# Recurrence gates of a hybrid decoder trunk: from both parts of the activations in separate matmuls to both parts stacked in one contraction

## The chip, the cores and the metric

The program runs on one core of one Trainium2 chip. The metric is device time in microseconds (us) of one execution. Engines are named as in the profile: PE is TensorE's matmul side and PEld its weight loads, DVE is VectorE, ACT is ScalarE, POOL is GpSimd, SP is SyncE, which issues the loads from memory. Every engine works its instructions in the order in which they stand in its own queue, and waits where an operand or a buffer is not yet free.

## The reference

Two layers, 256 tokens, width 1024. Each layer runs a SwiGLU feed-forward block, a mixing block, a second feed-forward block and a gated addition of a per-layer input. The change is in the mixing block, in the gates of its recurrence:

```python
def rg_lru(x, w_a, b_a, w_x, b_x, lam):
    xb = x.reshape(B, S, RNN_BLOCKS, RNN_BW)             # 16 blocks of 64 channels
    r = sigmoid(einsum('bsnc,ncd->bsnd', xb, w_a).reshape(B, S, C) + b_a)
    i = sigmoid(einsum('bsnc,ncd->bsnd', xb, w_x).reshape(B, S, C) + b_x)
    log_a = -RG_C * r * softplus(-lam)
    a = exp(log_a)
    mult = sqrt(-expm1(2.0 * log_a))
    u = mult * (i * x)
    h = associative_scan(h[t] = a[t] * h[t-1] + u[t])
```

So each of 16 blocks of 64 channels has two 64x64 gate matrices of its own. `x` here is the output of a causal convolution over the projected input. The other branch of the mixing block is an attention of 8 heads with q and k normalised per head; both branches go through output projections, are gated and added.

## The kernel before, in words

Activations lie with features on the 128 partitions and the 256 tokens in the free dimension: 8 feature tiles `m` of [128, 256]. All products are made in three terms so that they keep float32 accuracy: a value is split into a part `hi` (float32r) and the rest `lo`, and a product is hi x hi + hi x lo + lo x hi. The helper `mm3` (lines 308 to 310) issues these three matmuls of 256 columns; `mm3m` (lines 313 to 315) the same for token-major results.

Weights come through class `Weights`: SP loads a chunk into `wr`, ACT copies it into `wh` (line 94) and DVE subtracts to make `wl` (line 95), a unit of 1024 columns at a time, at most five units of each alive. A new unit can be written only when PE has finished the unit five before it. The number in a name (`wh107`) is the unit's.

In the mixing block (`mix`) the order written in the program is: projection to the recurrent branch with the convolution behind it (`conv`) and the split of its result `xc` (`split`, lines 524 and 525); the value projection `v` with the gates of tiles 0 to 4 between its chunks; four groups `qk_group` of the q and k projection, tokens on partitions, two for each half of the heads, with gates 5 to 7 in the first group. A qk group ends, for each of its two PSUM banks, with a square on ACT (line 657), a reduction and small steps on DVE and POOL (lines 659 to 663) and a scaling copy out of the bank (line 665).

After the first two qk groups `root` (line 572) takes one square root over all eight gate tiles on ACT, `tq`, with a load of ACT's function table before it; then `scan` multiplies (line 577) and runs the recurrence over the tokens (line 578), eight times each on DVE. Attention goes head by head in four steps: `step_a` transposes q and k and splits them (lines 700 to 704), `step_b` makes the scores `s` and the softmax (lines 717 to 723), `step_c` and `step_d` transpose the weights `pt` and make the output. Between them stand 24 projections called `filler`, each 24 matmuls of 256 columns into one PSUM bank `f`, the first eight of which are the other gate of the recurrent branch.

PSUM has four banks with the tag `mm` and four with `at`, given out in turn: a tile takes over the bank of the tile given out four earlier with its tag, and PE's first matmul into it waits until that one has been read. The first filler takes over the bank of `qk277`, the first bank of the third qk group.

The order on each engine is not the written one: a list scheduler of the framework moves instructions by its own estimate of times, so that a change in one place shifts others.

The gates of tile `m` before the change: for each of the two gates three matmuls with a 128x128 matrix that holds the two 64x64 blocks on its diagonal and zeros elsewhere, into one half each of a bank `g`; then two tanh on ACT (lines 556 and 557), `thr` and `thi`.

Of the kernel before, what the change touches and what calls it, by code (L numbers as in the profile page):

```python
# [16 lines left out]
P = 128  # L17
DEPTH = 2
D = 1024
KT = D // P            # feature tiles of the model width  # L20
S = 256
TT = S // P            # token tiles
FF = 2816
FT = FF // P           # feature tiles of the FFN width
# [4 lines left out]
# columns of the packed per-feature vectors (one column per feature tile)  # L29
# [11 lines left out]
VC = 258               # columns of one chunk of [v | f]  # L41
# [6 lines left out]
class Weights:  # L48
    """Weights in order of use: loaded in chunks, split into float32r parts hi + lo in units."""
# [11 lines left out]
    def load_first(self):  # L61
        """the first chunks in pieces: a list of loads, each to be issued in its place"""
# [34 lines left out]
    def apart(self, ap, n):  # L97
        """weights loaded and split out of turn, into buffers of their own"""
# [20 lines left out]
def trunk(ctx: ExitStack, tc: tile.TileContext, xT, pT, vec, w1i, w1o, wf, wqk, wv, wg, wro, wao, wo, w2i, w2o,  # L119
# [82 lines left out]
    # masks of S' = -S: +BIG where the key comes after the query  # L202
    mask = cp.tile([P, S], F32, name="mask")
    # cumulative sum over tokens: tri[t, t'] = 1 where t <= t'
    tri = cp.tile([P, S], F32R, name="tri")
    # selection columns for the forget bias: row groups (of 32) dk_hi, dk_lo, dq_hi, dq_lo
# [3 lines left out]
    sel = cp.tile([P, 3], F32, name="sel")      # [-lo rows | key rows | query rows]  # L210
# [6 lines left out]
    sp = cp.tile([P, DEPTH, 2, KT], F32, name="sp")   # [4 softplus(-lam) | its negative]  # L217

    def log_sigmoid(o, z, n):
        """o = min(z, 0) - log1p(exp(-|z|)) for [P, n], in steps"""  # L220
# [96 lines left out]
    class Pair:  # L317
        """tiles of [128, hi 256 | lo 256], four in each buffer"""
# [15 lines left out]
        def split(self, k, src, scale=None):  # L334
            """tile k = src (* scale) in two parts"""
# [9 lines left out]
    def mm2(ps, wh, wl, t, first, last):  # L345
        """ps[:, :256] + ps[:, 256:] += weights x activations, of which the second half is hi x lo"""
# [12 lines left out]
    def unit(ps, act):  # L359
        """one output tile [128 features, 256 tokens] from one weight unit of 8 tiles"""  # L360
        tiles(ps, W.next(), act, range(KT))
# [10 lines left out]
    def pair(psa, psb, act, between=None, tiles=tiles):  # L372
        """two units at the start of a stage, whose last input tile comes late"""
# [566 lines left out]
def _layout(inputs):  # L940
# [24 lines left out]
    for i, t in enumerate((g["rg_wa"], g["rg_wx"])):  # L965
        t = t.reshape(L, KT, 2, 64, 64)
        for b in range(2):
            wg[:, b * 64:(b + 1) * 64, :, i, b * 64:(b + 1) * 64] = t[:, :, b].transpose(0, 2, 1, 3)
# [49 lines left out]
```

## Time and profile before

| what | value |
|---|---|
| median of three runs | 1327.73 us (1326.57 to 1328.20) |
| span of the profiled execution | 1326.2 us |
| TensorE | busy 1313.2 us, 99% of the span, 8610 matmuls |
| VectorE | busy 1077.3 us, 81% |
| ScalarE | busy 814.1 us, 61% |

The profile gives the span from the first to the last instruction; the runs also hold what lies around it, so the fastest run is 0.4 us and the median 1.5 us above the span. A busy share over the whole span says little about one stage; the rows below are from the stage that the change touches, which in the first layer lies between about 205 and 440 us and in the second between about 857 and 1092 us.

### The profile page before, as it was taken

How to read it: one execution, taken by the hardware profiler on the slowest of the kernel's cores; microseconds unless marked ns; L12 is line 12 of the kernel's file. 1: busy time of each engine (PE TensorE's matmuls, PEld its weight loads, DVE VectorE, ACT ScalarE, POOL GpSimd, SP SyncE). 2: the span in 40 equal slices, each digit the busy share in tenths (PEclk: the TensorE clock that was granted, in tenths of full speed). 3: DMA queues.
4: the chain of work that ended last, by engine and by line, in shares of the span. 5: the costliest groups of instructions: out<-in, count | busy, mean ns of one | idle time of the engine just before them, and what ended most of it. 6: DMA issues, size and time to landing. Idle time of an engine off the chain costs nothing.

```text
span 1326.2 us, 22448 instructions
## 1 busy us (share of the span) xinstructions
PE 1313.2 (99%) x8610; PEld 1198.0 (90%) x8610; DVE 1077.3 (81%) x2139; ACT 814.1 (61%) x1467; POOL 35.8 (3%) x43
## 2 busy tenths in 40 slices
PE   8999999999999999999999999999999999999997
PEld 7888899989999888889988888998899998888897
DVE  7998768889768799867789877698997678998766
ACT  6665655867655666556556556578676556655643
POOL 1000000020000000000000000000200000000000
PEclk9999999999999999999999999999999999999998
DMA  7554565445345455456455546654443455554550
GB/s 278 199 186 159 194 229 190 159 151 207 142 145 191 156 212 190 165 173 240 168 189 188 185 141 226 219 189 159 170 177 139 154 183 203 184 187 153 207 192 33
DMA packets 37835, 239.16 MB, mean 180 GB/s; under 512 B 4320, under 2 KB 4960, under 8 KB 14944
## 3 DMA queue, kind: packets, MB, share of 16 engines
q1 hardware_dynamic: 37296, 237.21, 50.6%
q8 instruction: 68, 1.11, 0.3%
q10 hardware_dynamic: 432, 0.52, 0.1%
q14 instruction: 39, 0.32, 0.1%
HBM read 236.66 MB, written 1.05 MB: 179 GB/s over the span
## 4 chain that ended last, share of the span: by engine, by line
PE 98%; DMA 1%; DVE 0%; SPq 0%; ACT 0%; POOLq 0%; issue 0%; DVEq 0%
PE mm L351 20%; PE mm L349 11%; PE at L351 11%; PE at L349 6%; PE f L308 3%; PE f L310 3%; PE f L309 3%; PE qk L313 2%; PE qk L315 2%; PE qk L314 2%; PE mm L310 2%; PE mm L308 2%; PE mm L309 2%; PE mm L348 2%; PE ya L351 2%; PE at L348 2%
## 5 line engine op out<-in xcount | busy, mean ns | idle before, releaser
L94 ACT ACTIVATE wh<-wr 128x1024 fp32r<-128x1024 f32 (+3 forms) x482 | 471.5, 984 | 310.0 <-PE mm L351 90.9
L95 DVE TENSOR_TENSOR wl<-wr,wh 128x1024 fp32r<-128x1024 f32 (+3 forms) x482 | 542.8, 1128 | 143.5 <-ACT wh L94 138.4
L351 PE MATMUL at<-h,wh 128*128 128x512 f32 x616 | 219.8, 396 | 0.0
L351 PE MATMUL mm<-h,wh 128*128 128x512 f32 x616 | 219.1, 394 | 0.0
L349 PE MATMUL at<-h,wl 128*128 128x256 f32 x704 | 182.0, 281 | 2.8 <-DVE wl L95 2.8
L349 PE MATMUL mm<-h,wl 128*128 128x256 f32 x704 | 182.1, 280 | 0.0
L351 PE MATMUL mm<-f,wh 128*128 128x512 f32 x504 | 176.9, 394 | 0.0
L349 PE MATMUL mm<-f,wl 128*128 128x256 f32 x528 | 144.1, 280 | 0.0
L349 PEld LDWEIGHTS at<-h,wl 128*128 128x128 f32 x704 | 132.5, 189 | 11.6 <-ACT h L341 3.3
L349 PEld LDWEIGHTS mm<-h,wl 128*128 128x128 f32 x704 | 131.9, 188 | 8.1 <-DVE wl L95 0.3
L351 PEld LDWEIGHTS at<-h,wh 128*128 128x128 f32 x616 | 115.4, 189 | 22.7 <-DVE h L342 0.5
L351 PEld LDWEIGHTS mm<-h,wh 128*128 128x128 f32 x616 | 115.5, 188 | 22.4
L351 PEld LDWEIGHTS mm<-f,wh 128*128 128x128 f32 x504 | 94.4, 188 | 20.8
L308 PE MATMUL f<-h,wh 128*128 128x256 f32 x384 | 108.6, 283 | 0.0
L310 PE MATMUL f<-h,wl 128*128 128x256 f32 x384 | 108.5, 282 | 0.0
L309 PE MATMUL f<-h,wh 128*128 128x256 f32 x384 | 108.2, 282 | 0.0
L349 PEld LDWEIGHTS mm<-f,wl 128*128 128x128 f32 x528 | 99.4, 188 | 2.1
L309 PEld LDWEIGHTS f<-h,wh 128*128 128x128 f32 x384 | 72.3, 188 | 0.1
L308 PEld LDWEIGHTS f<-h,wh 128*128 128x128 f32 x384 | 72.3, 188 | 0.1
L310 PEld LDWEIGHTS f<-h,wl 128*128 128x128 f32 x384 | 72.3, 188 | 0.0
L385 ACT ACTIVATE sum<-mm 128x256 f32<-128x256 f32 x112 | 40.2, 375 | 50.7 <-PE mm L351 50.7
L386 DVE TENSOR_TENSOR sum<-mm,sum 128x256 f32<-128x256 f32 x112 | 45.0, 418 | 14.2 <-ACT sum L385 14.2
(287 smaller groups left out, 2848.4 us busy)
## 6 DMA issues: line engine op xcount, KB each, us to landing
wr<-in_w2i SPq DMA_DIRECT2D x44, 1024.0 KB, 4.8
wr<-in_w1i SPq DMA_DIRECT2D x42, 1024.0 KB, 4.8
wr<-in_wf SPq DMA_DIRECT2D x32, 1024.0 KB, 4.8
wr<-in_w1o SPq DMA_DIRECT2D x32, 704.0 KB, 4.0
wr<-in_w2o SPq DMA_DIRECT2D x32, 704.0 KB, 4.0
wr<-in_wqk SPq DMA_DIRECT2D x16, 1024.0 KB, 4.8
wr<-in_wv SPq DMA_DIRECT2D x8, 1032.0 KB, 4.8
wr<-in_wro SPq DMA_DIRECT2D x8, 1024.0 KB, 4.8
```

Source lines behind the costliest of these rows:

```text
L94: self.nc.scalar.activation(out=hi[:, c], in_=src[:, c], func=AF.Copy)
L95: self.nc.vector.tensor_tensor(out=lo[:, c], in0=src[:, c], in1=hi[:, c].bitcast(F32), op=ALU.subtract)
L308: T.matmul(ps, lhsT=wh, rhs=xh, start=first, stop=False)
L309: T.matmul(ps, lhsT=wh, rhs=xl, start=False, stop=False)
L310: T.matmul(ps, lhsT=wl, rhs=xh, start=False, stop=last)
L313: T.matmul(ps, lhsT=xh, rhs=wh, start=first, stop=False)
L314: T.matmul(ps, lhsT=xh, rhs=wl, start=False, stop=False)
L348: T.matmul(ps, lhsT=wh, rhs=t, start=True, stop=False, skip_group_check=True)
L349: T.matmul(ps[:, 0:S], lhsT=wl, rhs=t[:, 0:S], start=False, stop=False, skip_group_check=True)
L351: T.matmul(ps, lhsT=wh, rhs=t, start=False, stop=last, skip_group_check=True)
L385: A.activation(out=o, in_=ps[:, S:], func=AF.Copy)
L386: V.tensor_tensor(out=o, in0=ps[:, 0:S], in1=o, op=ALU.add)
```

## The change

The zeros of the block diagonal are dropped. For tile `m` and block `b` (64 channels) an operand `xs[b]` is made that has `hi` of the block's own channels in one half of the partitions and their `lo` in the other half. The weights are laid out on the host to match: the block's gate matrix stands twice in the rows, and the columns are both gates' 64 outputs side by side. One matmul with `wg_hi` then gives hi x hi + hi x lo for both gates, one with `wg_lo` gives the rest: two matmuls for each block, four for a tile where six stood. The results lie with the block's channels on the wrong or right half of the partitions, so `split` becomes two instructions on ACT and two on DVE of 64 partitions each, and the two tanh become four of 64 partitions each. Everything else is written as before.

```diff
-        xch = big([P, KT, S], F32R, "xch")
-        xcl = big([P, KT, S], F32R, "xcl")
+        xs = [big([P, KT, S], F32R, "xs") for _ in range(2)]
+        lower, upper = slice(0, 64), slice(64, P)
...
             def split():
-                A.activation(out=xch[:, m], in_=xc[:, m], func=AF.Copy)
-                V.tensor_tensor(out=xcl[:, m], in0=xc[:, m], in1=xch[:, m].bitcast(F32), op=ALU.subtract)
+                for b, own, other in ((0, lower, upper), (1, upper, lower)):
+                    A.activation(out=xs[b][own, m], in_=xc[own, m], func=AF.Copy)
+                    V.tensor_tensor(out=xs[b][other, m], in0=xc[own, m], in1=xs[b][own, m].bitcast(F32),
+                                    op=ALU.subtract)
             defer(conv, split)
...
         def gates(m):
             ps = two[m % 2]("g")
-            for g in range(2):
-                c = slice((m * 2 + g) * P, (m * 2 + g + 1) * P)
-                mm3(ps[:, g * S:(g + 1) * S], wg_hi[:, c], wg_lo[:, c], xch[:, m], xcl[:, m], True, True)
+            for b in range(2):
+                c = slice((m * 2 + b) * P, (m * 2 + b + 1) * P)
+                T.matmul(ps[:, b * S:(b + 1) * S], lhsT=wg_hi[:, c], rhs=xs[b][:, m], start=True, stop=False)
+                T.matmul(ps[:, b * S:(b + 1) * S], lhsT=wg_lo[:, c], rhs=xs[b][:, m], start=False, stop=True)
             thr, thi, th, a2 = work(s="thr"), work(s="thi"), work(s="th"), work(s="a2")
-            A.activation(out=thr, in_=ps[:, 0:S], func=AF.Tanh, scale=0.5, bias=hcol(l, "ba", m))
-            A.activation(out=thi, in_=ps[:, S:], func=AF.Tanh, scale=0.5, bias=hcol(l, "bx", m))
+            for b, own, other in ((0, lower, upper), (1, upper, lower)):
+                c = slice(b * S, (b + 1) * S)
+                A.activation(out=thr[own], in_=ps[own, c], func=AF.Tanh, scale=0.5, bias=hcol(l, "ba", m)[own])
+                A.activation(out=thi[own], in_=ps[other, c], func=AF.Tanh, scale=0.5, bias=hcol(l, "bx", m)[own])
...
-    wg = np.zeros((L, P, KT, 2, P), np.float32)
+    wg = np.zeros((L, 2, 64, KT, 2, 2, 64), np.float32)
...
-            wg[:, b * 64:(b + 1) * 64, :, i, b * 64:(b + 1) * 64] = t[:, :, b].transpose(0, 2, 1, 3)
+            wg[:, :, :, :, b, i ^ b] = t[:, :, b].transpose(0, 2, 1, 3)[:, None]
```

The scheduler then sets the engines' orders anew. Up to the gates the rows of all engines stand as before; behind them they differ through the rest of the mixing block, in both layers alike. In what follows line numbers of the changed kernel are those of its own file: lines 556 to 780 of the kernel before are 7 higher there (572 is 579, 577 is 584, 578 is 585, 657 to 665 are 664 to 672, 702 and 703 are 709 and 710, 717 is 724).

ScalarE, up to the square root over `tq` in the first layer. Before:

```order
L94 ACTIVATE wh101_3063<-wr50_3041 128x1024
L94 ACTIVATE wh102_3094<-wr51_3092 128x1024
L631 ACTIVATE dh268_3084<-dc267_3079 128x256
L563 ACTIVATE th246_2949<-thr244_2947,sp_113 128x256
L564 ACTIVATE a2247_2950<-a195_2514 128x256
L563 ACTIVATE th257_2991<-thr255_2989,sp_113 128x256
L564 ACTIVATE a2258_2992<-a195_2514 128x256
L94 ACTIVATE wh103_3116<-wr51_3092 128x1024
L572 ACT_TABLE_LOAD
L572 ACTIVATE tq196_2515<-tq196_2515,tiny_93 128x2048
```

And ScalarE at the same place now:

```order
L94 ACTIVATE wh106_3218<-wr53_3216 128x1024
L638 ACTIVATE dh268_3100<-dc267_3095 128x256
L570 ACTIVATE th246_2963<-thr244_2961,sp_113 128x256
L571 ACTIVATE a2247_2964<-a195_2526 128x256
L570 ACTIVATE th257_3005<-thr255_3003,sp_113 128x256
L571 ACTIVATE a2258_3006<-a195_2526 128x256
L94 ACTIVATE wh107_3238<-wr53_3216 128x1024
L664 ACTIVATE qsq279_3254<-qk277_3172 128x512
L579 ACT_TABLE_LOAD
L579 ACTIVATE tq196_2527<-tq196_2527,tiny_93 128x2048
```

The square root has moved behind weight unit 107 and behind the square of `qk277`, the first bank of the third qk group; before, it stood behind unit 103 and ahead of the squares of the second group (`qk265`, `qk266`).

VectorE behind the square root. Before, the last twelve rows up to the copy out of bank `qk277`:

```order
L665 TENSOR_TENSOR qk235_2884<-qk265_3039,s271_3137 128x512
L659 TENSOR_REDUCE s280_3240<-qsq279_3238 128x4
L95 TENSOR_TENSOR wl108_3265<-wr54_3262,wh108_3264 128x1024
L577 TENSOR_TENSOR tq196_2515<-tq196_2515,xc176_2202 128x256
L663 TENSOR_SCALAR s274_3146<-s274_3146,R183_2264 128x4
L660 TENSOR_SCALAR s280_3240<-s280_3240,s175_2201 128x4
L578 SCALAR_TENSOR_TENSOR xc176_2202<-a195_2514,tq196_2515 128x256
L665 TENSOR_TENSOR qk235_2884<-qk266_3040,s274_3146 128x512
L659 TENSOR_REDUCE s283_3249<-qsq282_3247 128x4
L663 TENSOR_SCALAR s281_3243<-s281_3243,R183_2264 128x4
L660 TENSOR_SCALAR s283_3249<-s283_3249,s175_2201 128x4
L665 TENSOR_TENSOR qk276_3155<-qk277_3156,s281_3243 128x512
```

VectorE now, behind the first five multiplications by the square root (line 584) and up to the splits of head 0's q and k:

```order
L666 TENSOR_REDUCE s280_3256<-qsq279_3254 128x4
L584 TENSOR_TENSOR tq196_2527<-tq196_2527,xc176_2202 128x256 x2
L585 SCALAR_TENSOR_TENSOR xc176_2202<-a195_2526,tq196_2527 128x256 x3
L95 TENSOR_TENSOR wl108_3281<-wr54_3278,wh108_3280 128x1024
L585 SCALAR_TENSOR_TENSOR xc176_2202<-a195_2526,tq196_2527 128x256
L584 TENSOR_TENSOR tq196_2527<-tq196_2527,xc176_2202 128x256
L585 SCALAR_TENSOR_TENSOR xc176_2202<-a195_2526,tq196_2527 128x256
L667 TENSOR_SCALAR s280_3256<-s280_3256,s175_2201 128x4
L95 TENSOR_TENSOR wl109_3312<-wr54_3278,wh109_3311 128x1024
L585 SCALAR_TENSOR_TENSOR xc176_2202<-a195_2526,tq196_2527 128x256 x2
L709 TENSOR_TENSOR aq289_3302<-tr287_3296,aq288_3301 128x256
L710 SCALAR_TENSOR_TENSOR aq291_3304<-tr287_3296,gqk_112,aq290_3303 128x256
```

VectorE goes on from there to the copy out of bank `qk277`:

```order
L95 TENSOR_TENSOR wl110_3349<-wr55_3346,wh110_3348 128x1024
L585 SCALAR_TENSOR_TENSOR xc176_2202<-a195_2526,tq196_2527 128x256
L666 TENSOR_REDUCE s283_3265<-qsq282_3263 128x4
L670 TENSOR_SCALAR s281_3259<-s281_3259,R183_2264 128x4
L95 TENSOR_TENSOR wl111_3373<-wr55_3346,wh111_3372 128x1024
L724 ISA pr294_3336,mx295_3337<-s293_3327,mask_100 128x128
L724 ISA mx295_3337 128x1
L724 ISA pr294_3336,mx295_3337<-s293_3327,mask_100 128x256
L724 ISA mx295_3337 128x1
L667 TENSOR_SCALAR s283_3265<-s283_3265,s175_2201 128x4
L95 TENSOR_TENSOR wl112_3435<-wr56_3432,wh112_3434 128x1024
L672 TENSOR_TENSOR qk276_3171<-qk277_3172,s281_3259 128x512
```

Head 0's splits and the first steps of its softmax have moved ahead of the copy out of bank `qk277`; before, the copy stood ahead of them.

TensorE at the first filler, which takes over the bank of `qk277`. Before:

```order
L314 MATMUL qk286_3261<-wl107_3223,h166_1935 128x512
L315 MATMUL qk286_3261<-wh107_3222,h166_1935 128x512
L308 MATMUL f314_3415<-h152_1632,wh108_3264 128x256
L309 MATMUL f314_3415<-h152_1632,wh108_3264 128x256
L310 MATMUL f314_3415<-h152_1632,wl108_3265 128x256
```

And TensorE there now:

```order
L308 MATMUL s293_3327<-aq290_3303,aq288_3301 128x128
L314 MATMUL qk286_3277<-wl107_3239,h166_1935 128x512
L315 MATMUL qk286_3277<-wh107_3238,h166_1935 128x512
L309 MATMUL s293_3327<-aq291_3304,aq288_3301 128x128
L310 MATMUL s293_3327<-aq290_3303,aq289_3302 128x128
L720 MATMUL s293_3327<-dk234_2899,aq292_3305 128x128
L308 MATMUL s293_3327<-aq290_3303,aq288_3301 128x256
L309 MATMUL s293_3327<-aq291_3304,aq288_3301 128x256
L310 MATMUL s293_3327<-aq290_3303,aq289_3302 128x256
L720 MATMUL s293_3327<-dk234_2899,aq292_3305 128x256
L308 MATMUL f314_3431<-h152_1632,wh108_3280 128x256
```

The eight score matmuls of head 0 (`s293`) now stand ahead of the first filler; before, they stood inside the first two fillers. The second of them reads `aq291`, which VectorE's line 710 writes.

## Rows read from the trace of the kernel before

**Rows 1.** The page: the span, the busy time of each engine, and the engines of the chain of work that ended last.

```profile
span 1326.2 us, 22448 instructions
PE 1313.2 (99%) x8610; PEld 1198.0 (90%) x8610; DVE 1077.3 (81%) x2139; ACT 814.1 (61%) x1467; POOL 35.8 (3%) x43
PE 98%; DMA 1%; DVE 0%; SPq 0%; ACT 0%; POOLq 0%; issue 0%; DVEq 0%
```

**Rows 2.** The waits of TensorE's matmuls over the whole span, the longest two of five: who waited for whom; us in total, times, longest.

```profile
PE at L349 <- DVE wl L95: 2.8, 2, 2.6
PE warm L873 <- POOL ones L193: 1.1, 1, 1.1
```

**Rows 3.** The matmuls of the gates, by the tile `g` they write: duration in ns (least/median/most), first and last start in us.

```profile
L308 PE MATMUL g<-xch,wbh x32: 276/280/287, 232.0 to 909.1; 128*128 128x256 f32 x32
L309 PE MATMUL g<-xcl,wbh x32: 277/281/288, 232.1 to 909.2; 128*128 128x256 f32 x32
L310 PE MATMUL g<-xch,wbl x32: 277/280/289, 232.2 to 909.3; 128*128 128x256 f32 x32
```

**Rows 4.** The timeline (start us, us, engine, line): the first of the twelve matmuls of gates 0 and 1, and the first matmul behind the twelve.

```profile
231.97 0.28 PE L308 MATMUL g<-xch,wbh 128*128 128x256 f32 x1
...
233.39 0.28 PE L313 MATMUL v<-wh,h 128*128 128x258 f32 x1
```

**Rows 5.** The steps on ACT and DVE that the change makes twice, by their lines: duration in ns (least/median/most), first and last start.

```profile
L524 ACT ACTIVATE xch<-xc x16: 396/408/428, 215.9 to 895.5; 128x256 fp32r<-128x256 f32 x16
L525 DVE TENSOR_TENSOR xcl<-xc,xch x16: 409/417/420, 217.8 to 896.5; 128x256 fp32r<-128x256 f32 x16
L556 ACT ACTIVATE thr<-g,half x16: 453/465/487, 233.8 to 909.9; 128x256 f32<-128x256 f32 x16
L557 ACT ACTIVATE thi<-g,half x16: 453/471/491, 234.2 to 910.2; 128x256 f32<-128x256 f32 x16
```

**Rows 6.** Busy us of each engine in stretches of 10 us over the gates (PE, PEld, DVE, ACT, POOL, then granted clock, DMA share, GB/s).

```profile
230.00:240.00 10.00, 10.00 (x86) 10.00 (x85) 9.29 (x20) 8.33 (x18) 0.00 (x0) 1.00 0.33 114
240.00:250.00 10.00, 10.00 (x74) 9.47 (x74) 8.22 (x17) 10.00 (x24) 0.00 (x0) 1.00 0.52 192
250.00:260.00 10.00, 10.00 (x53) 8.49 (x52) 8.66 (x31) 9.01 (x19) 0.00 (x0) 1.00 0.35 120
```

**Rows 7.** ScalarE's timeline around the square root; in brackets the idle time before a row and what ended it.

```profile
270.35 1.28 ACT L572 ACT_TABLE_LOAD   x1
271.64 2.01 ACT L572 ACTIVATE tq<-tq,tiny 128x2048 f32<-128x2048 f32 x1
273.56 1.06 ACT L657 ACTIVATE qsq<-qk 128x512 f32<-128x512 f32 x2
274.51 2.00 ACT L94 ACTIVATE wh<-wr 128x1024 fp32r<-128x1024 f32 x2
...
281.79 0.60 ACT L657 ACTIVATE qsq<-qk 128x512 f32<-128x512 f32 x1 [0.27 <-PE qk L315]
```

**Rows 8.** VectorE's timeline behind the square root (equal rows merged, xN).

```profile
273.68 2.44 DVE L577 TENSOR_TENSOR tq<-tq,xc 128x256 f32<-128x256 f32 x7 [2.10 <-ACT tq L572]
276.03 0.68 DVE L659 TENSOR_REDUCE s<-qsq 128x4 f32<-128x512 f32 x1
276.63 3.01 DVE L578 TENSOR_TENSOR_SCAN xc<-a,tq 128x256 f32<-128x256 f32 x5
279.56 1.20 DVE L95 TENSOR_TENSOR wl<-wr,wh 128x1024 fp32r<-128x1024 f32 x1
...
291.33 0.22 DVE L663 TENSOR_SCALAR s<-s,R 128x4 f32<-128x4 f32 x1
...
291.59 0.68 DVE L665 TENSOR_TENSOR qk<-qk,s 128x512 f32<-128x512 f32 x1
...
296.67 0.41 DVE L702 TENSOR_TENSOR aq<-tr,aq 128x256 fp32r<-128x256 f32 x1
297.00 0.47 DVE L703 SCALAR_TENSOR_TENSOR aq<-tr,gqk,aq 128x256 fp32r<-128x256 f32 x1
297.39 1.21 DVE L95 TENSOR_TENSOR wl<-wr,wh 128x1024 fp32r<-128x1024 f32 x1
298.52 0.68 DVE L659 TENSOR_REDUCE s<-qsq 128x4 f32<-128x512 f32 x1
```

**Rows 9.** VectorE's timeline at the first steps of head 0's softmax.

```profile
301.85 0.28 DVE L717 CUSTOM_DVE_ANT_0 pr<-s,mask 128x128 f32<-128x128 f32 x1
...
302.41 0.41 DVE L765 SCALAR_TENSOR_TENSOR sq<-sq,g 128x256 f32<-128x256 f32 x1
```

**Rows 10.** TensorE's timeline: the first matmul of the first filler, and head 0's second and last score matmul.

```profile
294.56 0.28 PE L308 MATMUL f<-h,wh 128*128 128x256 f32 x1
...
297.98 0.22 PE L309 MATMUL s<-aq,aq 128*128 128x128 f32 x1
...
298.67 0.28 PE L713 MATMUL s<-dk,aq 128*128 128x256 f32 x1
```

**Rows 11.** Stretches at the start of the program, columns as in rows 6.

```profile
8.00:12.00 4.00, 1.38 (x7) 0.80 (x6) 1.78 (x4) 2.29 (x6) 0.00 (x0) 1.00 0.97 336
12.00:15.40 3.40, 3.40 (x12) 2.92 (x12) 3.26 (x10) 3.40 (x9) 0.00 (x0) 0.50 1.04 422
```

## The prediction

> **What bounds the kernel now.** I read the page first: TensorE is busy for 99% of the span, and the chain that ended last is 98% TensorE [rows 1]. A busy PE need not be a full one, so I read its waits next: the longest in the whole span is 2.6 us, at the start, and no line waits more than 2.8 us in all [rows 2]. In the mixing block PE works without a gap. So a matmul less is time less, at the pace at which matmuls follow each other, and every wait that is new on PE is time more. The pace is not the 280 ns of a gate matmul's row [rows 3], since matmuls overlap: twelve of them start between 231.97 and 233.39, 0.118 us apart [rows 4].
>
> **What is removed.** 96 gate matmuls of 256 columns [rows 3] become 64: 2 blocks x 2 matmuls x 8 tiles x 2 layers. 32 x 0.118 = **3.8 us** less, 1.9 us in each layer.
>
> **What is added beside PE.** Per tile one more split on each of ACT and DVE and two more tanh. Instructions on 64 partitions do not occur on these lines before; their cost lies between half a row of 128 partitions (then nothing is added) and a full one. I take the full one, since nothing in a row says that a partition less saves time. Per layer that is 8 x 0.41 + 16 x 0.47 = 10.8 us on ACT and 8 x 0.42 = 3.4 us on DVE [rows 5]. The Trainium skill, page "ScalarE: Activation LUTs", section "What ACT_TABLE_LOAD costs", gives an activation a fixed part and 0.833 ns for each element of a lane, with no term for the partitions; by it 64 partitions cost what 128 do, an estimate of 0.49 us for 256 elements with a bias operand, and the trace's 0.47 us for 128 partitions fits that.
>
> ACT has room for little of it: between 230 and 260 us, where the tanh stand, it is busy for 27.3 of 30 us, and 7.5 us of tanh come on top [rows 5, 6]. So what ACT does behind the gates comes later, and the new order shows what: the square root in `root` now stands behind weight unit 107 and behind the square of bank `qk277`. This is where I see the price.
>
> **The square root against PE.** All times are those of the first layer in the trace. PE reaches a place behind the gates 16 x 0.118 = 1.9 us earlier than before. Before, the square root ended at 273.65 and the first filler started at 294.56 [rows 7, 10]: 20.9 us of room for DVE. Now ACT must first square `qk277`. That square began at 281.79 before, released by PE's last matmul into the bank [rows 7], so it can begin at 279.9 at the earliest. It takes 0.5 us (two in 0.95), the table 1.29, the root 2.01 [rows 7]: it ends at 279.9 + 0.5 + 1.3 + 2.0 = **283.7**. Whether 64-partition instructions are cheap does not matter to this time, since PE sets it.
>
> DVE waits for the root, as it did (2.10 us [rows 8]), and then works down its new rows. Paces from start to start [rows 8, 9]: line 577 0.336 us (seven in 2.35), 578 0.586 (five in 2.93), 659 0.60, 95 1.13, the small 660 and 663 0.13 each (two in 0.26), 702 0.33, 703 0.39, the pair at 717 0.56, and 665 0.68 to its end.
>
> - To the end of line 710, which makes what head 0's second score matmul reads: 8 x 0.336 + 7 x 0.586 + 0.60 + 2 x 1.13 + 0.13 + 0.33 + 0.39 = 10.5, and 0.1 to its end: 283.7 + 10.6 = **294.3**.
> - On to the copy out of `qk277`: 3 x 1.13 + 0.586 + 0.60 + 2 x 0.13 + 0.56 + 0.68 = 6.1: **300.3**.
>
> PE, if nothing held it, would start the first filler at 294.56 - 1.9 + 0.9 = 293.5; the 0.9 are the eight score matmuls that now stand ahead of it (the last seven took 0.8 from 297.98 on [rows 10]). Its second score matmul would come 0.8 earlier, at 292.7. So PE waits there for line 710, 294.3 - 292.7 = **1.6 us**. The filler's first matmul is then due at 295.1, but takes over the bank of `qk277`, which DVE has copied at 300.3: **5.2 us**. Before, this copy ended at 291.59 + 0.68 = 292.3 [rows 8], 2.3 us ahead of the filler. Everything on PE is queued behind the filler's first matmul: the transposes of head 0's softmax, all further fillers, and with them the release of weight buffers. Nothing on PE covers the wait.
>
> What is late next: the second bank `qk278` needs about 2 us more of DVE, the softmax of head 0 about 1.5; PE asks for both only after 23 matmuls, 2.7 us on. So they are in time, and the 6.8 us are paid once per layer. Both layers have the same rows in these stretches: 2 x 6.8 = **13.6 us**.
>
> **The clock.** At the start of the trace PE waited 2.6 us for a weight part [rows 2], and the next 3.4 us ran at a granted clock of 0.50, which is 1.2 GHz instead of 2.4 [rows 11]. 3.4 us at half speed lose 1.7 us. A wait of 5.2 us, with another just before it, is longer than that one, so I take one such drop per layer: **3.4 us**; the bounds are nothing and twice as much. The Trainium skill, "TensorE: Matmul & The Clock Gate", section "HAM oscillation — how this bites in real kernels", says that waits between bursts of matmuls send the array back to its low clock and are each paid again on the way up; rows 11 agree for one wait, no row shows one in this stage. By that rule the drop belongs in the sum; without it the sum is 3.4 us less.
>
> **The sum.** 1326.2 - 3.8 + 13.6 + 3.4 = 1339.4 us of span; the median of the runs is 1.5 above the span of the profile, so 1341.
>
> **The rivals.**
> 1. *The gain arrives whole.* The waits do not come up because DVE is 7 us earlier than my chain. For it: PE had no wait here before although the bank was free only 2.3 us ahead, so an order that the scheduler finds seems to fit. Against it: nothing in DVE's chain can shrink; each row has a measured pace, and its start hangs on PE's own matmul. 1327.7 - 3.8 = 1323.9.
> 2. *The waits come, the clock stays at 2.4 GHz.* 1341 - 3.4 = 1337.5. For it: only one drop is in the trace, at the start. Against: that wait was half as long.
> 3. *Half the waits.* The square of `qk277` or the DVE rows lie better by some 3 us per layer; the score wait vanishes and the bank's halves. 1327.7 - 3.8 + 2 x 3 = 1330, which is slower by 0.2%. The point from which the sign turns is a wait of 1.9 us per layer.
> 4. *More is late.* ACT carries 10.8 us more per layer, and heads 1 to 7 follow each other through ACT and DVE. One wait of 2 us more per layer, or a clock that stays low twice as long, gives 1345 to 1347.
>
> That the change doesn't do what it says can be left out: 64 gate matmuls stand in the new order.
>
> **How the numbers follow.** Forecast 0.43, rival 2 0.25, rival 4 0.13, rival 3 0.09 (two thirds of it slower, the rest near no change), rival 1 0.10. A difference under 0.2%, 2.7 us, can't be told from none by this measurement. Slower: 0.43 + 0.25 + 0.13 + 0.06 = 0.87; same 0.03; faster 0.10. The range leaves out rival 1, most of rival 3 and the far half of rival 4: 1331 to 1346 holds about 0.8. The forecast alone would be 1338 to 1344.
>
> **What would show it.** Right: 64 matmuls of `g` at 0.12 us each; the square root on ACT ends about 9.7 us ahead of where the first filler is due; PE's waits list two lines that it did not have, `s` waiting for DVE `aq` of line 710 (about 1.6 us, twice) and `f` waiting for DVE `qk` of line 672 (about 5 us, twice); in the stretch behind it the granted clock is below 1.00. Wrong: if the two waits are under 2 us per layer together, the chain on DVE broke, and the rows behind the square root would show at which step; if the waits are there and the clock is 1.00, only the last term falls; if PE waits in other places, more was late than I followed. Splits or tanh of 64 partitions at half the duration would leave this sum as it is.

## The result, and the profile after

The changed kernel takes 1344.32 us (1343.34 to 1345.09, four runs), the kernel before 1327.83 beside it (1326.57 to 1328.20): a ratio of 1.0124, with a 95% interval of 1.011 to 1.0137. It is slower, by 16.5 us. The profiled execution has a span of 1342.9 us, 16.7 more than in [rows 1].

The page first: span, busy time of the engines, and the engines of the chain that ended last.

```profile
span 1342.9 us, 22435 instructions
PE 1314.8 (98%) x8578; PEld 1198.9 (89%) x8578; DVE 1091.4 (81%) x2155; ACT 839.0 (62%) x1515; POOL 36.5 (3%) x43
PE 86%; ACT 7%; DVE 4%; issue 1%; DMA 1%; SPq 0%; POOLq 0%; DVEq 0%
```

PE has 32 matmuls less and yet is busy 1.6 us longer than in [rows 1]; the chain, 98% PE before, now runs for 11% through ACT and DVE. PE's waits, in the columns of [rows 2]:

```profile
PE f L308 <- DVE qk L672: 9.1, 2, 4.9
PE s L309 <- DVE aq L710: 6.4, 2, 3.2
PE at L349 <- ACT h L341: 2.1, 1, 2.1
```

The first two lines are new, each once per layer; the third lies at the start of the program, where [rows 2] have a wait on the same line for another releaser. The gates' matmuls, as in [rows 3], and the split and tanh lines, as in [rows 5]:

```profile
L557 PE MATMUL g<-xs,wbh x32: 278/281/289, 231.6 to 916.3; 128*128 128x256 f32 x32
L558 PE MATMUL g<-xs,wbl x32: 274/281/287, 231.7 to 916.4; 128*128 128x256 f32 x32
L526 ACT ACTIVATE xs<-xc x32: 397/415/422, 215.5 to 911.8; 64x256 fp32r<-64x256 f32 x32
L527 DVE TENSOR_TENSOR xs<-xc,xs x32: 418/420/422, 217.6 to 913.2; 64x256 fp32r<-64x256 f32 x32
L563 ACT ACTIVATE thr<-g,half x32: 453/470/472, 233.1 to 931.1; 64x256 f32<-64x256 f32 x32
L564 ACT ACTIVATE thi<-g,half x32: 466/472/478, 233.5 to 931.6; 64x256 f32<-64x256 f32 x32
```

64 matmuls of unchanged duration, and twice as many instructions on ACT and DVE that last on half the partitions as long as on all. PE's last matmul into `qk277`, and ScalarE around the square root, as in [rows 7]:

```profile
279.14 0.40 PE L315 MATMUL qk<-wh,h 128*128 128x512 f32 x1
...
279.90 0.41 ACT L571 ACTIVATE a<-a 128x256 f32<-128x256 f32 x1
280.21 1.05 ACT L94 ACTIVATE wh<-wr 128x1024 fp32r<-128x1024 f32 x1
281.16 0.58 ACT L664 ACTIVATE qsq<-qk 128x512 f32<-128x512 f32 x1
281.76 1.28 ACT L579 ACT_TABLE_LOAD   x1
283.05 2.01 ACT L579 ACTIVATE tq<-tq,tiny 128x2048 f32<-128x2048 f32 x1
```

No row of ACT has idle time ahead of it. The bank is complete at 279.54, but its square follows straight behind a weight unit at 281.16, 1.6 us later, and the root ends at 285.06, 11.4 us later than in [rows 7]. VectorE behind it, first and last rows of the chain that the prediction added up:

```profile
285.09 1.77 DVE L584 TENSOR_TENSOR tq<-tq,xc 128x256 f32<-128x256 f32 x5 [0.82 <-ACT tq L579]
...
295.19 0.47 DVE L710 SCALAR_TENSOR_TENSOR aq<-tr,gqk,aq 128x256 fp32r<-128x256 f32 x1
...
300.97 0.68 DVE L672 TENSOR_TENSOR qk<-qk,s 128x512 f32<-128x512 f32 x1
```

From the root's end to the end of line 710 there are 10.6 us, from there to the end of the copy out of `qk277` 6.0. TensorE at the same place, as in [rows 10]:

```profile
292.18 0.39 PE L315 MATMUL qk<-wh,h 128*128 128x512 f32 x1
295.71 0.48 PE L309 MATMUL s<-aq,aq 128*128 128x128 f32 x1 [3.15 <-DVE aq L710]
...
297.16 0.41 PE L720 MATMUL s<-dk,aq 128*128 128x256 f32 x1
301.71 0.58 PE L308 MATMUL f<-h,wh 128*128 128x256 f32 x1 [4.13 <-DVE qk L672]
...
305.08 0.31 PE L308 MATMUL f<-h,wh 128*128 128x256 f32 x1
```

The first filler starts 7.2 us later than in [rows 10]. The seven scores, 0.69 us from the second to the last in [rows 10], take 1.45; the first 15 filler matmuls, 0.118 us each in [rows 4], take 3.37, which is 0.22 each. The stretches, columns as in [rows 6], say why:

```profile
290.00:295.00 5.00, 2.57 (x12) 1.77 (x10) 5.00 (x9) 4.00 (x6) 2.21 (x1) 0.99 0.19 23
295.00:300.00 5.00, 1.86 (x7) 1.57 (x7) 5.00 (x13) 0.52 (x3) 0.17 (x1) 0.50 0.65 235
302.00:305.00 3.00, 3.00 (x15) 3.00 (x15) 3.00 (x11) 0.00 (x0) 1.67 (x2) 0.50 0.52 216
305.00:310.00 5.00, 5.00 (x44) 5.00 (x43) 3.87 (x9) 3.03 (x7) 0.58 (x1) 0.99 0.06 10
```

In this layer the granted clock is 0.50, 1.2 GHz, from the last us of the first wait on, and it is back at 2.4 GHz at about 305 us. In the second layer the scores still run at 2.4 GHz, and the clock is low only behind them:

```profile
955.00:957.00 2.00, 1.07 (x7) 0.87 (x7) 2.00 (x4) 0.00 (x0) 0.00 (x0) 1.00 0.86 365
961.00:967.00 6.00, 5.74 (x27) 5.74 (x28) 4.55 (x14) 0.36 (x1) 2.72 (x3) 0.50 0.36 141
```
```profile
961.26 0.58 PE L308 MATMUL f<-h,wh 128*128 128x256 f32 x1 [4.93 <-DVE qk L672]
...
966.34 0.84 PE L738 MATMUL pt<-ident,pr 128*128 128x128 f32 x3
```

There 23 filler matmuls take 5.08 us, again 0.22 each, and the transposes behind them still start at the low clock. In the first layer ACT is idle for most of 295 to 300 while DVE is full: DVE is now what PE waits for.

### The profile page after: what moved, and what is told of

It is laid out like the page before. It is cut to its first block, busy times and chain, and to the rows that moved or that the text cites. A ratio compares the mean times of both kernels' runs of the same rounds, so it can differ in the third digit from the quotient of the medians.

```text
span 1342.9 us, 22435 instructions
## 1 busy us (share of the span) xinstructions
PE 1314.8 (98%) x8578; PEld 1198.9 (89%) x8578; DVE 1091.4 (81%) x2155; ACT 839.0 (62%) x1515; POOL 36.5 (3%) x43
## 4 chain that ended last, share of the span: by engine, by line
PE 86%; ACT 7%; DVE 4%; issue 1%; DMA 1%; SPq 0%; POOLq 0%; DVEq 0%
PE mm L351 19%; PE mm L349 11%; PE at L351 11%; PE at L349 6%; PE f L308 4%; PE f L310 3%; PE f L309 3%; ACT wh L94 2%; PE mm L308 2%; PE mm L310 2%; PE mm L309 2%; PE mm L348 2%; PE ya L351 2%; PE at L348 2%; PE o L351 1%; PE pl L308 1%
## 5 line engine op out<-in xcount | busy, mean ns | idle before, releaser
L308 PE MATMUL f<-h,wh 128*128 128x256 f32 x384 | 110.2, 287 | 9.1 <-DVE qk L672 9.1
L309 PE MATMUL f<-h,wh 128*128 128x256 f32 x384 | 110.1, 287 | 0.0
L308 PEld LDWEIGHTS f<-h,wh 128*128 128x128 f32 x384 | 74.2, 193 | 9.6 <-DVE qk L672 9.6
L309 PEld LDWEIGHTS f<-h,wh 128*128 128x128 f32 x384 | 74.2, 193 | 0.0
```

The lines of the kernel that those rows point to most:

```text
L308: T.matmul(ps, lhsT=wh, rhs=xh, start=first, stop=False)
L309: T.matmul(ps, lhsT=wh, rhs=xl, start=False, stop=False)
```

## The experiments

Times are medians; unless said otherwise each is held against the kernel before on the same chip, between 1327.5 and 1328.3 us. A wait "2, 0.6" came twice, once per layer, the longest 0.6 us.

**The scans out of the way.** First theory: the eight multiplications and eight scans stand on DVE ahead of the copy, so queue them behind the copies out of all four banks of the third and fourth group.

```diff
-                V.tensor_tensor(out=dst[:, w, t].rearrange("p (h d) -> p h d", h=4),
+                cp_ins = V.tensor_tensor(out=dst[:, w, t].rearrange("p (h d) -> p h d", h=4),
...
-                if w == 0:
-                    scan(2 * u)
-                    scan(2 * u + 1)
...
+            if f < KT:
+                with tc.issue_after(out_of[3].ins):
+                    scan(f)
```

> The changed kernel with one edit: the sixteen DVE instructions of the scans (lines 584 and 585) are queued on DVE behind the copies out of the four banks of the third and fourth qk group. ACT's order up to the square root, the 64 matmuls, the splits and the tanh stay. If the price is DVE's order (7.4 us of scan rows, 8 x 0.336 + 8 x 0.586, ahead of head 0's split and of the copy out of qk277), the copy ends near 290 instead of 301.65, the waits of PE for lines 710 and 672 vanish, the granted clock stays 1.00, and the time is 1327.8 - 3.8 = 1324. If the added work of ACT and DVE is itself the price, the waits come back in another place (the banks of the fourth group, or the softmax) and the time stays above 1335. Between them: the scans compete with the weight splits among the fillers, and 2 to 4 us of new waits give 1326 to 1328.

Measured: 1334.27 us, ratio 1.0047 (1.0035 to 1.006), 10 us under the changed kernel but 6.4 over the one before. The copy out of `qk277` now starts at 288.88 and the first filler at 291.21, with no wait. Five smaller pairs of waits came in place of the two large ones, 7.0 us together, the largest `o` for DVE (2, 1.3) and `ya` for a weight unit (2, 0.9). With the 3.8 us of the matmuls taken off they explain 3.2 of the 6.4; the other 3 us stand in no listed wait. So the rows ahead of the copy on DVE made the two large waits, and the scans have no free place behind the copies either. A control did the same to the kernel before.

> The kernel before with the edit of the first experiment alone: the scans queued on DVE behind the copies out of the four banks. It is the control of that run, which came out at 1334.3 with waits of its own (0.56 us at the third bank, 0.57 and 0.88 us at `ya`, 1.3 us at the last projection `o`, per layer). If these come from the moved scans, they stand here too and the time is 1331 to 1334. If they come from the added work of the splits and tanh, this gives 1327.8.

Measured: 1332.29 us, ratio 1.003 (1.0019 to 1.0041), with `pt` waiting for DVE (2, 0.8): 4.1 us are the price of the moved scans themselves, and not of the change.

**The matmuls alone.** The 64 matmuls stay; the split and the two tanh are again one instruction of 128 partitions each. This kernel leaves out the stacking of `hi` and `lo`, so its gates do not get the right operands, and only its time is of use.

```diff
-                for b, own, other in ((0, lower, upper), (1, upper, lower)):
...
+                A.activation(out=xs[0][:, m], in_=xc[:, m], func=AF.Copy)
+                V.tensor_tensor(out=xs[1][:, m], in0=xc[:, m], in1=xs[0][:, m].bitcast(F32), op=ALU.subtract)
...
+            A.activation(out=thr, in_=ps[:, 0:S], func=AF.Tanh, scale=0.5, bias=hcol(l, "ba", m))
+            A.activation(out=thi, in_=ps[:, S:], func=AF.Tanh, scale=0.5, bias=hcol(l, "bx", m))
```

> The changed kernel with its 64 gate matmuls, but with one split (one ACT, one DVE instruction of 128 partitions) and two tanh of 128 partitions per tile, as before; the operands of the gates are therefore not the right ones, and only the time is of use. If the price comes from the added ACT and DVE instructions, this gives the gain whole: no wait on lines 710 and 672, 1327.8 - 3.8 = 1324. If the stacked matmuls or their earlier end were the cause, the waits stay and the time is 1338 to 1344.

Measured: 1327.98 us, ratio 1.0002 (0.9993 to 1.0011). The large waits are gone, so the added instructions made them. But the 3.8 us did not arrive either. PE's waits:

```profile
PE ya L348 <- ACT wh L94: 1.7, 2, 0.9
PE f L308 <- DVE qk L668: 0.9, 2, 0.4
```

and ACT at the weight unit that `ya` waited for:

```profile
389.62 1.06 ACT L94 ACTIVATE wh<-wr 128x1024 fp32r<-128x1024 f32 x1 [1.72 <-PE ya L351]
```

ACT sat idle until PE had released the buffer. The order had changed here too: the first matmul of one more unit of the projection `ya` stood ahead of the first of `yb`. To get the old order at `ya` without touching a matmul, the next kernel gives the splits of q and k ten buffers instead of five (and takes four from other tags for the room), which leads the scheduler to another order.

```diff
-        return kp.tile([P, 256], dt, name=nm(s), tag="w", bufs=12)
+        return kp.tile([P, 256], dt, name=nm(s), tag="w", bufs=9)
-        return kp.tile([P, 512], dt, name=nm(s), tag="w2", bufs=3)
+        return kp.tile([P, 512], dt, name=nm(s), tag="w2", bufs=2)
...
-            s["q"] = qh, ql = awork(S, "aq", 5), awork(S, "aq", 5)
+            s["q"] = qh, ql = awork(S, "aq", 10), awork(S, "aq", 10)
```

> The run with the matmuls alone again (full splits, two tanh of 128 partitions, operands of the gates not the right ones), with ten buffers `aq` instead of five, nine `w` instead of twelve, two `w2` instead of three. With these the scheduler leaves the rows at the first output projection `ya` as they stood in the kernel before: no third `ya` unit is put ahead of the first `yb`. If that unit, whose weights were 0.87 us late, is where 1.3 us per layer of the matmuls' gain went, this gives 1328.0 - 2.6 = 1325.4, with the 0.4 us at the first filler left. If the heads of attention are late anyhow, TensorE waits at `yb` instead and the time stays 1328.

Measured: 1324.74 us, ratio 0.9976 (0.9966 to 0.9985), 3.5 us faster than before. The wait at `ya` is gone, the one at `f` (2, 0.4) is left. The worth of the matmuls is clearer from PE's timeline: from the first gate matmul to the last matmul into `qk277` PE takes 1.8 us less than before in the first layer and 1.9 in the second, in this run, in the one before it and in the changed kernel alike, and 0.0 to 0.2 less in the runs that keep 96 gate matmuls. So the matmuls are worth what they were counted at, and the order behind them decides how much of it is left. Of the 3.8 us between the two profiled executions here, 1.4 lie ahead of the gates and 2.4 behind. The kernel before with these buffers was not run, so what they do by themselves is not shown.

**The load alone.** The kernel before with its 96 matmuls, the split and the tanh each in two instructions of 64 partitions, operands in place.

```diff
+                for h in (slice(0, 64), slice(64, P)):
+                    A.activation(out=xch[h, m], in_=xc[h, m], func=AF.Copy)
...
+            for h in (slice(0, 64), slice(64, P)):
+                A.activation(out=thr[h], in_=ps[h, 0:S], func=AF.Tanh, scale=0.5, bias=hcol(l, "ba", m)[h])
```

> The kernel before with its 96 gate matmuls, but with each split and each tanh made in two instructions of 64 partitions, in place. If the added instructions make the price, the square root comes late here too, PE waits at head 0's scores and at the first filler, and the time is 1327.8 plus the 15.4 us of waits and 5.7 us of low clock that the changed kernel shows, less up to 3.8 us by which PE asks later: 1345 to 1349. If they lie in ACT's gaps, 1328. The tanh of 64 partitions should stand 0.48 us apart as in the changed kernel if the partitions decide, and 0.36 us as before if only the shift from one half to the other does.

Measured: 1339.55 us, ratio 1.0094 (1.0078 to 1.0109): 11.7 of the loss without any change to PE's work, though less than the 17 to 21 us that were expected.

```profile
PE f L308 <- DVE qk L667: 7.4, 2, 3.7
```

The root ends at 282.73 here, 9.1 us later than in [rows 7], and PE's last matmul into `qk277` is not earlier than before: ACT's load moved the root, not PE's pace. The scores stand ahead of the filler here too, but more qk matmuls stand between the first and the second of them: the second starts at 294.67, and line 705 (710 in the changed kernel) ends at 294.46, so PE does not wait for it.

**A busy PE in the wait.** The changed kernel with 28 matmuls of 128 columns ahead of head 0's scores and 38 behind them, written into columns of the score bank that nothing reads; the order of PE in this block is fixed by hand.

```diff
+                    if h == 0 and t == 0:
+                        for _ in range(28):
+                            T.matmul(ps[:, 384:512], lhsT=qh[:, q], rhs=kh[:, 0:P], start=True, stop=True)
...
+                if h == 0:
+                    for _ in range(38):
+                        T.matmul(ps[:, 384:512], lhsT=qh[:, 0:P], rhs=kh[:, 0:P], start=True, stop=True)
```

> The changed kernel with 28 matmuls of 128 columns ahead of head 0's scores and 38 behind them, into columns 384 to 511 of the score bank that nothing reads, so that TensorE works through most of its two waits. The waits' ends stay where DVE sets them, but DVE's softmax of head 0 moves behind the copy out of qk277, which can end 0.56 us earlier. If the low clock behind the waits is lost time of its own (5.7 us in both layers by the balance of the two traces), the granted clock stays near 1.00 and the time is 1344.3 - 5.7 - 1.1 = 1337.5. If the low clock costs nothing beyond the waits, 1343. If the added matmuls run past the waits, the time rises by what they run over.

Measured: 1340.23 us, ratio 1.0106 (1.0084 to 1.0128; one of the four runs took 1347.31), 4.1 us less than the changed kernel with 132 matmuls more, where 6.8 less were expected. The stretch that had a clock of 0.50, and PE's timeline:

```profile
295.00:300.00 5.00, 5.00 (x45) 5.00 (x45) 5.00 (x11) 0.00 (x0) 1.05 (x2) 1.00 0.57 187
```
```profile
290.82 3.24 PE L722 MATMUL s<-aq,aq 128*128 128x128 f32 x28
...
295.59 4.36 PE L727 MATMUL s<-aq,aq 128*128 128x128 f32 x38
300.30 0.28 PE L308 MATMUL f<-h,wh 128*128 128x256 f32 x1
```

The clock stays at 2.4 GHz. From the first gate matmul to the first `o` of layer 1 PE takes 2.0 us less than in the changed kernel, and from there to the first `o` of layer 2 another 2.6 less. Not all of these 4.5 us are the clock, since DVE's order changed as well: the softmax and a weight split now stand behind the copy out of `qk277`, which ends at 298.93, 1.7 us earlier counted from the first gate matmul. The added matmuls run past it, so that of this the first filler starts 0.4 us earlier in each layer. The 3.8 us that are left are put down to the clock; the rows of the changed kernel show 4.4 us lost to it behind the filler's start. (Of the 6.1 us between the two spans 1.0 lies ahead of the gates and 0.5 behind the first `o` of layer 2.)

**Less on ACT.** If ACT's backlog sets the root, taking work from ACT must bring it forward: first the squares `a2` to POOL, then the copies of `hi` too.

```diff
-                A.activation(out=a2, in_=at[:, m], func=AF.Square)
+                G.tensor_tensor(out=a2, in0=at[:, m], in1=at[:, m], op=ALU.mult)
```

> The changed kernel with the square `a2` of each gate tile (line 571, 8 x 0.31 us of ACT per layer) made on POOL instead of ACT. If ACT's backlog sets the square root, the root ends some 3 us earlier than 285.06 (2.5 us of squares, and it no longer stands behind the 0.5 us square of qk277), DVE reaches line 710 near 292.5 and the copy out of qk277 near 297 (8 x 0.336 + 8 x 0.586 + 4 x 1.13 and 3 us of other rows behind the root), so the score wait vanishes, the first filler waits about 3 instead of 4.1 to 4.9 us, and the time is 1344.3 - 2 x 4.5 - 2 = 1333. If TensorE's last matmul into qk277 sets the root, as the prediction took it, at most 1 us per layer is gained: 1342.

```diff
-                    A.activation(out=xs[b][own, m], in_=xc[own, m], func=AF.Copy)
+                    G.tensor_copy(out=xs[b][own, m], in_=xc[own, m])
```

> As the run with `a2` on POOL, and the copies that make `hi` in `split` (line 526, 16 per layer, 0.33 to 0.41 us each on ACT) on POOL too, so that ACT has less to do than in the kernel before. If ACT's load is the first cause, the root ends near 279 and the waits shrink further, to about 2 us per layer: 1330 to 1333. If DVE's order alone decides, no more is gained than by the run before it: 1333 to 1335. If POOL is too slow for the operands of the gates, TensorE waits in the value projection and the time is above 1336.

Measured: 1337.86 us (ratio 1.0069, 1.0054 to 1.0084) and 1334.58 (1.0045, 1.003 to 1.006). Both times are above what was expected (1333, and 1330 to 1333). The root ends at 282.89 and at 278.01, against 285.06, in both ahead of the square of `qk277` again; in the second run the first gate matmul is 1.7 us early already (229.83 against 231.56), so that counted from there the root is 2.1 and 5.3 us earlier; the wait at `s` shrinks from 3.2 to 1.2 and 0.8 us a layer, the one at `f` from 4.9 to 3.2 and stays there. ACT in the second of the two:

```profile
276.00 2.01 ACT L579 ACTIVATE tq<-tq,tiny 128x2048 f32<-128x2048 f32 x1 [1.18 <-DVE tq L574]
```

Now ACT waits for DVE: ACT's backlog is gone, and a wait of 3.2 us for DVE's copy is left. I put it down to DVE's second subtraction per tile and its scans; no run takes the subtraction alone away. The next runs treat both engines.

**Both, and where the scans stand.** Scans 0 to 3 are written one behind each step of the third group, scans 4 to 7 queued on DVE behind the copies out of that group's two banks: once with everything left on ACT, once with `a2` and `hi` on POOL, and once, with both on POOL, in the kernel before.

```diff
-                    scan(2 * u)
-                    scan(2 * u + 1)
+                    for m in range(4 * u // 4, 4 * (u + 1) // 4):
+                        scan(m)
+                elif u == 0:
+                    with tc.issue_after(out_of[1].ins):
+                        for m in range(4, KT):
+                            scan(m)
```

> The changed kernel with scans 4 to 7 queued behind the copies of the third group alone, ACT's work as it is. The root ends at 285.06 as before; line 710 at 285.06 + 4 x 0.336 + 4 x 0.586 + 2 x 0.6 + 2 x 1.13 + 1.0 = 293.2 and the copy out of qk277 2 us later. The score wait shrinks to 0.7 us, that of the first filler to 1.1, too short for a low clock, and a third `ya` unit stands ahead of `yb`, which cost 1.3 us per layer where it was seen: 1327.9 - 3.8 + 2 x 3.1 = 1330. If ACT's load is what counts and DVE's order is a detail, the time stays above 1338.

> The changed kernel with ACT's load cut as in the run before (`a2` and the copies of `hi` on POOL) and scans 4 to 7 queued on DVE behind the copies out of the two banks of the third group (scans 0 to 3 stay). Both causes are then met: the root ends near 278 as in that run (TensorE 2.1 us early from the start of the program there), and ahead of the copy out of qk277 four scans, four multiplications and two weight splits fewer stand (2.3 + 1.3 + 2.3 us), so the copy ends near 290, before the first filler is due at 291.5. No wait on lines 710 and 672, the rows at `ya` stand as in the kernel before, and the time is 1327.9 - 3.8 = 1324. If the late scans cost as in the control of the first experiment (1.7 us per layer), 1327.5. If the waits only move, 1330 or more.

> The control: the kernel before with the same two moves (squares `a2` and the copies `xch` on POOL, scans 4 to 7 behind the copies of the third group), with its 96 gate matmuls. It has no waits that these could take away, so 1327.9 if they cost nothing. What the run with both moves on the changed kernel gains over this one is the worth of the change where its price is gone: 3.8 us by the count of matmuls.

Measured: 1335.56 us with ACT as it was (ratio 1.0058, 1.0044 to 1.0072), its waits in the mixing block spread over `f`, `s`, `ya` and `pt`, none above 1.1 us and 6.8 together, with which 1330 was expected: some 5 us stand in no listed wait; 1329.05 with POOL (1.0009, 1.0000 to 1.0018); 1326.86 for the kernel before (0.9997, 0.9988 to 1.0006), where the moves neither cost nor bring anything. With POOL the waits at `s` and at the first filler are gone, and one is new:

```profile
PE f L308 <- ACT pr L729: 3.9, 2, 1.9
```

The line names ACT's `pr`, which had long been done. The bank that the third filler takes over was read last by DVE, in a row that ended at 301.30; the filler starts at 301.45:

```profile
297.90 1.26 DVE L585 TENSOR_TENSOR_SCAN xc<-a,tq 128x256 f32<-128x256 f32 x2
...
299.75 1.22 DVE L95 TENSOR_TENSOR wl<-wr,wh 128x1024 fp32r<-128x1024 f32 x1
300.88 0.42 DVE L771 TENSOR_TENSOR g<-f,RB 128x256 f32<-128x256 f32 x1
```

Ahead of it stood the four scans just moved. So they were spread: scan 4 + f behind the copy out of filler f, for f from 0 to 3.

```diff
-            V.tensor_tensor(out=g, in0=ps[:, 0:S], in1=n.RB, op=ALU.mult)
+            g_ins = V.tensor_tensor(out=g, in0=ps[:, 0:S], in1=n.RB, op=ALU.mult)
+            if f < KT - 4:
+                with tc.issue_after(g_ins.ins):
+                    scan(4 + f)
```

> The changed kernel, its whole computation kept, with the squares a2 and the copies of hi on POOL as in the run with both on POOL, scans 0 to 3 written one behind each step of the third group, and scans 4 to 7 queued on VectorE one each behind the copies out of the banks of fillers 0 to 3, and no longer all four behind the copies of the third group. In the run with all four there, only one wait of size was left, 1.95 us per layer at the third filler, for the bank of the first filler, whose last reader on VectorE stood behind the four scans (3.7 us), head 0's softmax and weight splits; the time was 1329.05. Theory that this queue is the last of the price: with the scans spread the reader comes some 3 us earlier, the wait goes, and with it the low clock behind it: 1329.05 - 2 x 1.95 - about 1 = 1324, which is before minus the 3.8 us of the matmuls. Rival, VectorE has no slack at all between 278 and 305 us: the four scans then delay head 1's splits or later copies, the wait moves to other lines of PE at about the same size, and the time stays at 1327 to 1330.

Measured: **1322.64 us** (1321.64 to 1322.78), ratio 0.996 (0.9947 to 0.9974): faster than both kernels, with the whole computation in it.

```profile
span 1321.0 us, 22479 instructions
PE 1308.8 (99%) x8578; PEld 1194.0 (90%) x8578; DVE 1091.7 (83%) x2155; ACT 820.9 (62%) x1467; POOL 67.4 (5%) x91
```
```profile
290.45 0.69 DVE L672 TENSOR_TENSOR qk<-qk,s 128x512 f32<-128x512 f32 x1
...
298.34 0.40 DVE L768 TENSOR_TENSOR g<-f,RB 128x256 f32<-128x256 f32 x1
298.66 0.41 DVE L584 TENSOR_TENSOR tq<-tq,xc 128x256 f32<-128x256 f32 x1
```

The copy out of `qk277` ends at 291.14 and the first filler starts at 293.06; its bank is read at 298.34, 2.5 us earlier than in the run before. PE has no listed wait in the mixing block, and the clock is 1.00 in every stretch from 285 to 310 us. The rival of that run, that DVE has no slack at all, fell. The gain is 5.4 us where the matmuls explain 3.8; 0.5 of the rest lies at the start of the program and about 1 us is not accounted for, 0.6 of it behind the first `o` of layer 2. The same spreading in the kernel before was not tried, so how much of the 5.4 the change brings by itself is not shown.

## Why the prediction was right, point by point

The span was forecast at 1339.4 us and came out at 1342.9. The 3.5 us between them are 1.8 more of waits and 2.1 more of what was counted for the clock, less 0.4 at the start.

- **The 3.8 us of the matmuls: right.** From the first gate matmul to the last matmul into `qk277` PE gains 1.8 us in the first layer and 1.9 in the second, against 1.9 counted. The run with the matmuls alone and the old order at `ya` is 3.5 us faster, 2.4 of it behind the gates by its trace.
- **Full price for half the partitions: right for the duration, short for ACT's load.** 470 and 472 ns for the tanh, 415 for the copy, 420 for the subtraction, close to [rows 5]. By the Trainium skill, page "ScalarE: Activation LUTs", section "What ACT_TABLE_LOAD costs", the time of an activation hangs on the elements of a lane and not on the lanes; the trace agrees. But I took durations as a pace, and ACT's instructions overlap: see the last section. The tanh of a layer cost 8 x (4 x 0.48 - 2 x 0.36) = 9.6 us more on ACT, where I counted 7.5.
- **The square root: the step that was mis-sized.** I put its end at 283.7, set by PE's last matmul into `qk277`, and wrote that the price of the 64-partition instructions does not matter to it. It ended at 285.06, and no idle time stands ahead of the square: ACT's backlog set it. The two runs with work taken from ACT brought the root forward by 2.1 and 5.3 us, counted from the first gate matmul, and the run with the load alone put it at 282.73. That the number came out near is luck: the square began at 281.16, only 1.3 us behind the 279.9 that PE allowed by the prediction's count, so the wrong engine gave nearly the right time.
- **DVE's chain behind it: right.** 10.6 us to line 710 and 6.0 on to the copy, as added up; both ends are late by the root's 1.35 us (295.66 and 301.65 against 294.3 and 300.3).
- **The two waits: right in place, 15.4 us instead of 13.6.** At `s` 3.15 and 3.23 for 1.6, from the late root; at `f` 4.13 and 4.93 for 5.2. The 0.8 us between the layers are the scores: at half clock, in the first layer, they used up that part of the wait.
- **The clock: right in kind, 5.2 us instead of 3.4.** The balance of the profiled execution: 16.7 us more of span = -0.4 ahead of the gates - 3.8 + 15.4 of waits + 5.5 left over. Of these 5.5 the rows of the first layer show 1.45 - 0.69 = 0.8 at the scores and 3.37 - 15 x 0.118 = 1.6 at the fillers, those of the second 5.08 - 23 x 0.118 = 2.4 at the fillers and 0.5 at the transposes; the last 0.3 are in no row. One drop per layer was right, but it cost 2.4 and 2.8 us where I took 1.7. The Trainium skill, "TensorE: Matmul & The Clock Gate", section "HAM oscillation — how this bites in real kernels", says that a wait between bursts of matmuls is paid for again, in a cold start of the burst behind it; here it holds, and the run that kept PE busy got 3.8 us back.
- **Later banks in time: right.** No wait behind the first filler is listed for the mixing block.
- **The rivals.** "The gain arrives whole" was refuted by the two waits; "the clock stays" by the stretch at 0.50; "half the waits" by 7.3 and 8.2 us per layer. Its turning point, a wait of 1.9 us per layer, was met by the run with POOL and the half scans: 1.95 us per layer, and a time that can't be told from before.

## What to carry to other kernels

With the matrix engine at 99%, a matmul saved pays at its pace, but work moved to the engines that feed it pays by what stands in their queues ahead of the next bank: follow the row that last reads the bank, and count the room ahead of the waiting matmul, not the average busy share. A rewrite of some instructions reorders others far away, so a small gain is seen only when the order at every later bank still fits; here moving 24 small instructions of a layer to an idle engine and spreading four scans turned 16.5 us of loss into 5.4 of gain. Waits of some us on TensorE have a second price behind them, in the clock: here 2.4 and 2.8 us behind the two waits of a layer.

## What the hardware showed beyond that

**The pace of ACT's tanh.** In the kernel before, two rows of 128 partitions follow each other in 0.36 us although each lasts 0.47 (233.79 and 234.15). In the changed kernel, where each reads or writes another half of the partitions than the one ahead of it, they follow in 0.48:

```profile
235.91 0.47 ACT L563 ACTIVATE thr<-g,half 64x256 f32<-64x256 f32 x1
236.39 0.47 ACT L564 ACTIVATE thi<-g,half 64x256 f32<-64x256 f32 x1
236.87 0.47 ACT L563 ACTIVATE thr<-g,half 64x256 f32<-64x256 f32 x1
```

In the run with the load alone the pairs stay in one half, and the pace alternates, 0.38 within a half and 0.47 on the change:

```profile
236.10 0.47 ACT L558 ACTIVATE thr<-g,half 64x256 f32<-64x256 f32 x1
236.48 0.46 ACT L559 ACTIVATE thi<-g,half 64x256 f32<-64x256 f32 x1
236.95 0.47 ACT L558 ACTIVATE thr<-g,half 64x256 f32<-64x256 f32 x1
```

So the overlap of two activations is lost when the half changes, in these rows; the cause was not looked for.

**POOL's times scatter.** The 64x256 copy that ACT does in 0.40 to 0.42 us took 0.39 to 1.34 on POOL in the run with both moved there, the 128x256 square 0.61 to 1.59. In the control, the kernel before with both on POOL, it cost nothing (1326.86 us against 1327.52).
